# Attention scores with split keys: the second pass over 128 rows, with zeros beside the low parts, in place of a pass over 64

## Chip, core and metric

The kernel runs as one program on one core of a Trainium2 chip. The metric is the time of one execution in device microseconds (us). TensorE (PE in the profile) multiplies matrices; a weight load (PEld) puts the stationary operand in place ahead of each matmul. VectorE (DVE), ScalarE (ACT) and GpSimd (POOL) work on tiles; SyncE (SP) issues nearly all DMAs. A pass here is one matmul instruction with its weight load; its pitch is the time from its start to the start of the next instruction on PE.

## What is computed

Four layers over 512 tokens of width 1024, in fp32: a mixer with short convolution and forgetting attention, a conformer convolution, an HGRN2 mixer and a sliding-window attention, each followed by a feed-forward layer. The change touches the scores of the two attentions. Heads are 64 wide.

```python
# forgetting attention (layer 0): 8 heads, blocks of 128 queries, all earlier keys
s = einsum("bqhd,bkhd->bhqk", q[:, start:end], k[:, :end]) * 64 ** -0.5
s = where(mask, s + bias, -inf); p = softmax(s)
outs.append(einsum("bhqk,bkhd->bqhd", p, v[:, :end]))
...
# sliding window attention (last layer): 16 query heads on 2 key heads, blocks of 128 queries x 256 keys
scores = einsum('bnqkgd,bnskd->bnkgqs', q, kb) * 64 ** -0.5
scores = where(valid, scores - slopes * dist, -inf)
out = einsum('bnkgqs,bnskd->bnqkgd', softmax_with_sink(scores), vb)
```

## The kernel before

**Precision by splitting.** Matmuls run in a rounded 32-bit type. To keep fp32 accuracy a value is split into a high part (the rounded copy) and a low part (value minus copy), and a product takes three passes: high by high, high by low, low by high. `mm3` (lines 537 to 541) does this for all projections: L539, L540 and L541 are its three passes, on tiles named fm, tm and op.

**Scores.** A head has only 64 rows, half of the 128 that a matmul can contract over. So `stack_q` puts, for head i of a pair (i is 0 or 1), the high part of q in one half of the rows and the low part in the other, and `stack_k` copies the high part of k to both halves. `mm_s` then needs two passes:

```python
T.matmul(out, lhsT=q[:, i, qs], rhs=k[:, i, ks], start=True, stop=False)               # L845
T.matmul(out, lhsT=q[HALF[i], i, qs], rhs=kl[HALF[i], ks], start=False, stop=True)     # L846
```

L845 contracts over 128 rows (high q and low q, each by high k). L846 contracts over 64 rows, rows 0 to 63 for i = 0 and 64 to 127 for i = 1 (high q by low k). The low parts of both heads of a pair lie in one tile kl of 128 by 512.

**Attention in layer 0.** `fox_worker` (three of them run interleaved) goes over 8 heads and 4 blocks of queries: `mm_s` into a bank S, bias and maximum on DVE (L940), exponential on ACT (L944), scaling on DVE (L947), transposes on PE (L956, bank PT), high and low copy of the transposed weights (L530 on ACT, L531 on DVE, tile PTs), then the product with v (L973, bank O), and two copies into osb (L979 on ACT, L982 on DVE). When a pair of heads is done, `collect` splits it (L530, L531, tile y) and frees its q, k and kl. Scores are 128, 256, 384 or 512 wide, 8 pairs of passes each. Between these stand the projections of later heads, and at the end the output projection (op), which goes through its weights in units: first the first half of the columns for units 0 to 3, then the second half for units 0 to 2, and so on.

**Sliding window.** `att` does the same for 8 pairs of heads and two halves of the sequence: 8 passes in a row per half (L845 and L846 in turn, 256 wide, or 128 wide at the sequence's start), then bias and maximum on DVE (L1708), exponentials on ACT (L1720), transposes on PE (L1732), copies on ACT (L1734) and the product with v (L1743). There are 64 pairs of passes: 16 of 128 wide and 48 of 256.

**What sets the order.** A planner in the kernel's file (`Sched`) runs all of this as tasks. Each operation has a fixed cost in a formula; the planner takes the one that could start first and emits it, so the order on every engine is fixed when the kernel is built. Buffers come from pools with a fixed number of slots: `spool` has 34 slots of 4 KB per partition, shared by weights, q, k, PTs, y and others, `tpool` has 8 of 2 KB. A weight unit takes three slots in turn: wr (the DMA's target), wh (high part, L498 on ACT) and wl (low part, L507 on DVE). Where the planner expects PE to stand idle for more than 0.6 us, and a bank is free, it puts matmuls of zeros there (`warm`, L1880).

A tile kl comes from `tpool` in layer 0 and from `spool` in the sliding window.

Of the kernel before, what the change touches and what calls it, by code (L numbers as in the profile page):

```python
# [8 lines left out]
F32 = mybir.dt.float32  # L9
F32R = mybir.dt.float32r  # L10
U8 = mybir.dt.uint8
AF = mybir.ActivationFunctionType
ALU = mybir.AluOpType
# [386 lines left out]
def program(nc, tc, ap, tp, debug=None):  # L400
    S = Sched()
    V, A, G, T = nc.vector, nc.scalar, nc.gpsimd, nc.tensor
    spool = Pool(tp["s"], "s", N_SLOTS)
    tpool = Pool(tp["t2"], "t2", N_T2)
# [7 lines left out]
    def dve(n, fn, reads, writes, fast=False, aps=0):  # L412
        return Op("DVE", 0.069 + n * (0.00052 if fast else 0.00104) + 0.061 * aps, fn, reads, writes)

    def act(n, fn, reads, writes, table=None, extra=0.0, psum=False):
        return Op("ACT", (0.05 if psum else 0.093) + n * 0.000833 + extra, fn, reads, writes, table=table)
# [10 lines left out]
    def slot(shape=(128, 1024), dtype=F32, name="s", need=1):  # L427
        return Alloc(spool, list(shape), dtype, name, need=need)
# [7 lines left out]
    def bank(name="b", need=1):  # L436
        return Alloc(ppool, [128, 512], F32, name, need=need)

    def free(*bs):
        for b in bs:  # L440
            b.pool.put(b)
# [70 lines left out]
    def get_w():  # L512
        u = W.cur
        W.cur += 1
        yield Wait(lambda: u in W.lo)
        W.gone += 1
        return W.hi.pop(u), W.lo.pop(u)
# [305 lines left out]

    HALF = (slice(0, 64), slice(64, 128))

    def stack_q(q, b):
        for i in range(2):
            s_, o_ = HALF[i], HALF[1 - i]  # L830
            yield act(512, lambda: A.activation(out=q[s_, i, :], in_=b[s_, :], func=AF.Copy, scale=0.125), (b,), (q,), psum=True)
# [4 lines left out]
    def stack_k(k, kl, b):  # L836
        for i in range(2):
            s_, o_ = HALF[i], HALF[1 - i]
            yield act(512, lambda: A.activation(out=k[s_, i, :], in_=b[s_, :], func=AF.Copy), (b,), (k,), psum=True)
            yield act(512, lambda: A.activation(out=k[o_, i, :], in_=b[s_, :], func=AF.Copy), (b,), (k,), psum=True)  # L840
            yield dve(512, lambda: V.tensor_tensor(out=kl[s_, :], in0=b[s_, :], in1=k[s_, i, :].bitcast(F32), op=ALU.subtract), (b,), (kl,))
        free(b)

    def mm_s(out, q, k, kl, i, qs, ks):
        T.matmul(out, lhsT=q[:, i, qs], rhs=k[:, i, ks], start=True, stop=False)  # L845
        T.matmul(out, lhsT=q[HALF[i], i, qs], rhs=kl[HALF[i], ks], start=False, stop=True)  # L846


    def short_conv(ct, gc, xa, gb, ys):
# [57 lines left out]
    def fox_worker(env, qk, osb, heads, done):  # L907


        for hd in heads:  # L910
# [14 lines left out]
            for pr in range(2):  # L925
# [51 lines left out]
                ts_ = slice(256 * pr, 256 * pr + 256)  # L977
                s_, o_ = HALF[par], HALF[1 - par]
                yield act(256, lambda: A.activation(out=ob[s_, ts_], in_=b2[o_, :256], func=AF.Copy), (b2,), (ob,), psum=True)  # L979
# [27 lines left out]
    def layer0_mixer():  # L1007
        env, qk, osb, ys = {}, {}, {}, {}
        spool.reserve = RES[0] + BASE

        def qk_copy(i, qb_, kb_):
            q = yield slot((128, 2, 512), F32R, "q", need=4)
            yield from stack_q(q, qb_)
            k = yield slot((128, 2, 512), F32R, "k", need=4)
            kl = yield Alloc(tpool, [128, 512], F32R, "kl", need=2)
            yield from stack_k(k, kl, kb_)
            qk[i] = (q, k, kl)

        vv = []

        def v_room():
            for i in range(4):
                vv.append((yield slot((128, 8, 128), F32R, "v", need=4)))

        def v_copy(n, tb, b):
            yield Wait(lambda: len(vv) == 4)
            t = vv[tb]
            src = b[:, :256].rearrange("p (h d) -> p h d", d=64)
            y = [t[:, 4 * n:4 * n + 4, 64 * i:64 * i + 64] for i in range(2)]
            yield from split(src, b, y, t, n=256, psum=True)  # L1030
            free(b)
            if all(x.need <= 0 for x in vv):
                env["v"] = vv

        S.spawn(v_room(), -5, "v")

        def v_part(n, cuts):

            bs, k = [], 0
            for m in cuts:  # L1040
                w = yield from get_w()
                for tb in range(4):
                    if k == 0:
                        bs.append((yield bank("tm", need=8)))
                    b, ts_ = bs[tb], slice(128 * tb, 128 * tb + 128)
                    for i in range(m):
                        ki, cs = k + i, slice(n * i, n * i + n)
                        yield pe(3 * n / 2400, lambda: mm3(b[:, :n], (xh[:, ki, ts_], xl[:, ki, ts_]), (w[0][:, cs], w[1][:, cs]), ki == 0, ki == 7),
                                 [w[0], w[1], X.blocks[tb][ki // 4]], [b])
                free(*w)  # L1050
                k += m
            return bs

        def gates(bs):

            g = yield t2("fg", (128, 4, 8), need=4)
            for tb in range(4):
                yield dve(8, lambda: V.tensor_copy(out=g[:, tb, :], in_=bs[tb][:, 256:264]), (bs[tb],), (g,))
            for tb in range(4):
                S.spawn(v_copy(0, tb, bs[tb]), -5, "v")  # L1060
            b = yield bank("fT")

            def tr():
                for tb in range(4):
                    T.transpose(b[:8, 128 * tb:128 * tb + 128], g[:, tb, :], ident)
            yield pe(0.436, tr, (g, bident), (b,))
            free(g)
            yield from fox_decay(b, env)

        bs = yield from fm_quads(4)  # L1070
        S.spawn(qk_copy(0, bs[0], bs[1]), -5, "qk")
        S.spawn(qk_copy(1, bs[2], bs[3]), -5, "qk")
        bs = yield from v_part(264, (3, 3, 2))
        S.spawn(gates(bs), -6, "decay")
        bs = yield from v_part(256, (4, 4))
        for tb in range(4):
            S.spawn(v_copy(1, tb, bs[tb]), -5, "v")

        left = [2] * 4

        def done(i):
            left[i] -= 1

        for i in range(FOX_WORKERS):
            S.spawn(fox_worker(env, qk, osb, range(i, 8, FOX_WORKERS), done), -4, f"fox{i}")

        def collect(i):
            yield Wait(lambda: left[i] == 0)
            y = osb[i]
            y.need = 0  # L1090
            p = yield slot((128, 2, 512), F32R, "y", need=2)
            yield from split(y.t, y, (p[:, 0, :], p[:, 1, :]), p)
            free(y)
            ys[4 + i] = p
            free(*qk[i], env["nck"][i])
            if sum(left) == 0:
                free(*vv)

        for i in range(4):
            S.spawn(collect(i), -5, f"y{i}")  # L1100
        got = {}
        for n, c in P1_FM_TAIL:
            got[n, c] = yield from fm_unit()
            if n == "k":
                S.spawn(qk_copy(c, got["q", c], got["k", c]), -5, "qk")
            elif n == "gb":
                S.spawn(short_conv(c, got["gc", c], got["xa", c], got["gb", c], ys), -5, "sconv")
        chain, blocks = boundary(B("mix_post0", "ffn_pre0"), "h0m")
        yield from out_proj([lambda k=k: ys.get(k) for k in P2_ORDER], chain, P=PQ[0][0], Q=PQ[0][1])
        X.blocks = blocks  # L1110
# [528 lines left out]
    def swa(kv_blocks_done):  # L1639
        ys, qs, osb, env = {}, {}, {}, {}  # L1640
# [15 lines left out]
        def kv_epi(k, v):  # L1656
            nonlocal vs
            ks = yield slot((128, 2, 512), F32R, "k", need=4)
            s = yield slot((128, 2, 512), F32, "kl", need=1)
            kl = yield slot((128, 512), F32R, "kl", need=2)  # L1660
            env["kv"] = s
            vs = s[:, 1, :].rearrange("p (a b) -> p a b", b=128)
            yield from stack_k(ks, kl, k)
            env["k"], env["klo"] = ks, kl
            t = yield t2("vT")
            yield dve(512, lambda: V.tensor_copy(out=t.t, in_=v.t), (v,), (t,))
            free(v)
            b = yield bank("vt")

            def tr():  # L1670
                for i in range(4):
                    T.transpose(b[:, 128 * i:128 * i + 128], t[:, 128 * i:128 * i + 128], ident)
            yield pe(0.436, tr, (t, bident), (b,))
            free(t)
            yield act(512, lambda: A.activation(out=s[:, 1, :], in_=b.t, func=AF.Copy), (b,), (bv, s), psum=True)
            free(b)
# [92 lines left out]
        for a in range(2, 8):  # L1769
            b = yield from fm_unit()  # L1770
# [174 lines left out]
```

## Time and profile before

| | us |
|---|---|
| median of 3 runs | 2363.87 (2362.8 to 2363.88) |
| the profiled execution | 2366.44 |
| its span | 2364.6 |
| PE busy | 2345.2 (99%) |
| PE weight loads busy | 1979.6 (84%) |
| DVE busy | 1198.5 (51%) |
| ACT busy | 911.8 (39%) |
| POOL busy | 129.3 (5%) |
| share of PE in the chain that ended last | 96% |

Busy time of an engine counts the time that instructions are in it. Matmuls overlap, so a busy PE need not be a PE at its peak: what a matmul costs is read from its pitch, not from its duration.

### The profile page before, as it was taken

What the parts mean: (1) busy time and instruction counts of PE and PEld (TensorE: products, weight loads), DVE (VectorE), ACT (ScalarE), POOL (GpSimd) and SP (SyncE); (2) the same over time, 40 slices, a digit from 0 to 9 for tenths busy, and PEclk for the clock granted to TensorE, in tenths of its full rate; (3) what the DMA queues carried; (4) which work ended last, traced back from release to release, by engine and by line L of the source; (5) the groups of instructions that cost most, each with busy time, mean ns of one, the idle gap of its engine ahead of it and who ended that gap; (6) DMA issues with size and microseconds to landing.
All of it is one profiled execution on the core that took longest, in us unless ns stands there. A gap on an engine that the chain in (4) does not pass through costs nothing.

```text
span 2364.6 us, 29469 instructions
## 1 busy us (share of the span) xinstructions
PE 2345.2 (99%) x11828; PEld 1979.6 (84%) x11828; DVE 1198.5 (51%) x2038; ACT 911.8 (39%) x1614; POOL 129.3 (5%) x152
## 2 busy tenths in 40 slices
PE   9999999999999999999999999999999999999998
PEld 9778988888878988888988889888888788888887
DVE  5776533333787533323656875444345445444432
ACT  6454323222466332322543544333323554333331
POOL 0000000000383000000000000000000000000000
PEclk9999999999999999999999999999999899999999
DMA  5223322232343222233221122222342013222240
GB/s 185 99 73 115 117 72 89 89 130 94 120 149 115 99 81 89 72 125 125 81 98 54 63 97 91 80 77 85 116 151 81 10 46 115 95 75 72 98 143 36
DMA packets 62936, 224.68 MB, mean 95 GB/s; under 512 B 6984, under 2 KB 7240, under 8 KB 62800
## 3 DMA queue, kind: packets, MB, share of 16 engines
q1 hardware_dynamic: 62368, 222.41, 27.4%
q8 instruction: 93, 1.52, 0.3%
q10 hardware_dynamic: 432, 0.40, 0.1%
q14 instruction: 43, 0.35, 0.0%
HBM read 220.67 MB, written 2.11 MB: 94 GB/s over the span
## 4 chain that ended last, share of the span: by engine, by line
PE 96%; DVE 1%; POOL 1%; ACT 1%; DMA 0%; issue 0%; SPq 0%; POOLq 0%; ACTq 0%; DVEq 0%
PE fm L539 18%; PE fm L541 18%; PE fm L540 18%; PE op L539 9%; PE op L541 9%; PE op L540 9%; PE tm L539 2%; PE tm L541 2%; PE tm L540 2%; PE S L846 1%; PE xt L689 1%; PE O L1743 1%; PE S L845 1%; PE S L1506 1%; POOL cy L1188 1%; PE o L1569 1%
## 5 line engine op out<-in xcount | busy, mean ns | idle before, releaser
L539 PE MATMUL fm<-xh,wh 128*128 128x512 f32 (+1 forms) x2160 | 799.6, 370 | 0.0
L541 PE MATMUL fm<-xh,wl 128*128 128x512 f32 (+1 forms) x2160 | 789.2, 365 | 0.0
L540 PE MATMUL fm<-xl,wh 128*128 128x512 f32 (+1 forms) x2160 | 789.2, 365 | 0.0
L507 DVE TENSOR_TENSOR wl<-wr,wh 128x1024 fp32r<-128x1024 f32 x379 | 457.1, 1231 | 286.6 <-ACT wh L498 180.7
L498 ACT ACTIVATE wh<-wr 128x1024 fp32r<-128x1024 f32 x379 | 387.3, 1051 | 261.7 <-DMA wr<-wall 128.4
L541 PEld LDWEIGHTS fm<-xh,wl 128*128 128x128 f32 x2160 | 409.0, 189 | 65.9
L539 PEld LDWEIGHTS fm<-xh,wh 128*128 128x128 f32 x2160 | 409.7, 190 | 65.0 <-issue 2.5
L540 PEld LDWEIGHTS fm<-xl,wh 128*128 128x128 f32 x2160 | 409.7, 190 | 61.4
L539 PE MATMUL op<-wh,p 128*128 128x512 f32 x704 | 274.9, 390 | 0.4 <-DVE sg L805 0.4
L541 PE MATMUL op<-wh,p 128*128 128x512 f32 x704 | 274.0, 389 | 0.0
L540 PE MATMUL op<-wl,p 128*128 128x512 f32 x704 | 273.9, 389 | 0.0
L805 DVE TENSOR_TENSOR sg<-fm,sg 128x512 f32<-128x512 f32 x88 | 60.9, 692 | 383.3 <-PE fm L541 376.2
L530 ACT ACTIVATE p<-sg 128x512 fp32r<-128x512 f32 x88 | 55.6, 632 | 357.4 <-DVE sg L805 357.4
L539 PEld LDWEIGHTS op<-wh,p 128*128 128x128 f32 x704 | 132.2, 188 | 28.2 <-DVE sg L805 0.9
L541 PEld LDWEIGHTS op<-wh,p 128*128 128x128 f32 x704 | 132.1, 188 | 27.5
L540 PEld LDWEIGHTS op<-wl,p 128*128 128x128 f32 x704 | 132.2, 188 | 27.1
L660 POOL TENSOR_TENSOR ss<-ss,mhalf 128x1 f32<-128x1 f32 x48 | 26.1, 543 | 1449.7 <-DVE ss L655 1443.1
L539 PE MATMUL op<-wh,y 128*128 128x512 f32 x256 | 102.8, 402 | 0.2 <-DVE y L1002 0.2
L541 PE MATMUL op<-wh,y 128*128 128x512 f32 x256 | 100.0, 391 | 0.0
L540 PE MATMUL op<-wl,y 128*128 128x512 f32 x256 | 99.8, 390 | 0.0
L531 DVE TENSOR_TENSOR p<-sg,p 128x512 fp32r<-128x512 f32 x88 | 60.9, 693 | 61.4 <-ACT p L530 61.4
L1188 POOL TENSOR_TENSOR cy<-cp,cy 128x512 f32<-128x512 f32 x60 | 86.1, 1436 | 30.1 <-ACT cp L1187 26.1
(246 smaller groups left out, 2277.5 us busy)
## 6 DMA issues: line engine op xcount, KB each, us to landing
wr<-wall SPq DMA_DIRECT2D x379, 512.0 KB, 3.5
row<-rows SPq DMA_DIRECT2D x14, 512.0 KB, 3.7
cm<-cmat SPq DMA_DIRECT2D x14, 512.0 KB, 4.6
h<-x SPq DMA_DIRECT2D x8, 256.0 KB, 7.2
nck<-negc SPq DMA_DIRECT2D x4, 512.0 KB, 5.6
alibi<-alibi SPq DMA_DIRECT2D x4, 512.0 KB, 4.9
out<-out SPq DMA_DIRECT2D x8, 256.0 KB, 2.3
mk<-masks SPq DMA_DIRECT2D x2, 288.0 KB, 5.1
```

The costliest lines, as they stand in the source:

```text
L498: yield act(1024, lambda: A.activation(out=b.t, in_=r.t, func=AF.Copy), (r,), (b,))
L507: yield dve(1024, lambda: V.tensor_tensor(out=b.t, in0=r.t, in1=hh.t.bitcast(F32), op=ALU.subtract), (r, hh), (b,))
L530: yield act(n, lambda: A.activation(out=y0, in_=raw, func=AF.Copy), (rb,), (yb,), psum=psum)
L531: yield dve(n, lambda: V.tensor_tensor(out=y1, in0=raw, in1=y0.bitcast(F32), op=ALU.subtract), (rb,), (yb,))
L539: T.matmul(out, lhsT=a[0], rhs=b[0], start=s, stop=False)
L540: T.matmul(out, lhsT=a[0], rhs=b[1], start=False, stop=False)
L541: T.matmul(out, lhsT=a[1], rhs=b[0], start=False, stop=e)
L660: yield Op("POOL", 0.29 + 0.167 * cols, lambda: G.tensor_tensor(out=ss[:, 8:8 + cols], in0=ss[:, 4:4 + cols], in1=mhalf[:, :cols], op=ALU. ...
L689: T.transpose(b[:, 128 * i:128 * i + 128], n[:, c:c + 128], ident)
L805: yield dve(512, lambda: V.tensor_tensor(out=c.t, in0=u.t, in1=c.t, op=ALU.mult), (u, c), (c,))
L845: T.matmul(out, lhsT=q[:, i, qs], rhs=k[:, i, ks], start=True, stop=False)
L1188: yield pool(512, lambda: G.tensor_tensor(out=y.t, in0=p.t, in1=y.t, op=ALU.add), (p,), (y,))
```

## The change

The tile kl gets two planes like k, one for each head of the pair. The plane of head i holds the low part of k in that head's half of the rows, and zeros in the other half, written by a memset on GpSimd. The second pass of `mm_s` then contracts over all 128 rows, with the same stationary operand as the first; the zeros take out the product with the low part of q. kl doubles in size, and in layer 0 it moves from `tpool` to `spool`.

```diff
     def stack_k(k, kl, b):
...
-            yield dve(512, lambda: V.tensor_tensor(out=kl[s_, :], in0=b[s_, :], in1=k[s_, i, :].bitcast(F32), op=ALU.subtract), (b,), (kl,))
+            yield dve(512, lambda: V.tensor_tensor(out=kl[s_, i, :], in0=b[s_, :], in1=k[s_, i, :].bitcast(F32), op=ALU.subtract), (b,), (kl,))
+            yield Op("POOL", 0.5, lambda: G.memset(kl[o_, i, :].bitcast(F32), 0.0), (), (kl,))
...
     def mm_s(out, q, k, kl, i, qs, ks):
         T.matmul(out, lhsT=q[:, i, qs], rhs=k[:, i, ks], start=True, stop=False)
-        T.matmul(out, lhsT=q[HALF[i], i, qs], rhs=kl[HALF[i], ks], start=False, stop=True)
+        T.matmul(out, lhsT=q[:, i, qs], rhs=kl[:, i, ks], start=False, stop=True)
...
-            kl = yield Alloc(tpool, [128, 512], F32R, "kl", need=2)
+            kl = yield slot((128, 2, 512), F32R, "kl", need=4)
...
-            kl = yield slot((128, 512), F32R, "kl", need=2)
+            kl = yield slot((128, 2, 512), F32R, "kl", need=4)
```

In the changed file the two passes are lines 847 and 848, the memset is line 843, and later lines move by two. The planner makes a new order from it. On PE, DVE and ACT the order differs inside the attention of layer 0 only; in the sliding window no matmul changes its place.

The end of layer 0's attention on PE before: the last scores, the first half of the columns of the output projection for unit 3 (weights 1923 and 1925), transposes, and the last product with v.

```order
L845 MATMUL S_2053<-k_1766,q_1743 128x512
L846 MATMUL S_2053<-kl_1767,q_1743 128x512
...
L541 MATMUL op_2011<-wh_1837,y_1285 128x512
L539 MATMUL op_1975<-wh_1923,y_1566 128x512
L540 MATMUL op_1975<-wl_1925,y_1566 128x512
...
L956 MATMUL PT_2030<-ident,B_2040 128x128 x2
L539 MATMUL op_2000<-wh_1923,y_1566 128x512
...
L541 MATMUL op_2108<-wh_1683,y_1032 128x512
L973 MATMUL O_2110<-PTs_2094,v_92 128x256 x2
```

The same place on PE after (the four op groups of unit 3 now use weights 2129 and 2148):

```order
L847 MATMUL S_2058<-k_1785,q_1757 128x512
L848 MATMUL S_2058<-kl_1786,q_1757 128x512
...
L541 MATMUL op_2011<-wh_1901,y_1258 128x512
L1882 MATMUL warm_2089<-zeros 128x128 x3
L958 MATMUL PT_2026<-ident,B_2036 128x128 x2
...
L1882 MATMUL warm_2104<-zeros 128x128 x9
L975 MATMUL O_2103<-PTs_2097,v_92 128x256 x2
...
L1882 MATMUL warm_2157<-zeros 128x128 x18
L539 MATMUL op_1974<-wh_2129,y_1544 128x512
```

Five op groups of three passes that stood among the last transposes and products now stand behind them, with three runs of warm matmuls in their place.

The end of layer 0's attention on ACT, before: the high part of unit 3's weights (1923) is made well ahead of the last copies.

```order
L530 ACTIVATE PTs_1899<-PT_1848 128x384
L498 ACTIVATE wh_1923<-wr_1921 128x1024
L979 ACTIVATE osb_1786<-O_1907 64x256
...
L979 ACTIVATE osb_1786<-O_2110 64x256
L530 ACTIVATE y_2129<-osb_1786 128x512
L498 ACTIVATE wh_2141<-wr_2139 128x1024
```

On ACT after:

```order
L530 ACTIVATE PTs_2100<-PT_2027 128x384
L981 ACTIVATE osb_1811<-O_2103 64x256
L530 ACTIVATE y_2124<-osb_1811 128x512
L498 ACTIVATE wh_2129<-wr_2127 128x1024
```

The high part of unit 3's weights (2129) now stands behind the last copy of the attention's output and its split.

## Rows read from the trace of the kernel before

**Rows 1.** Busy PE, PEld, DVE, ACT, POOL (x instructions), PEclk, DMA: layer 0's attention, sliding window.
```profile
70.00:200.00 130.00, 129.25 (x613) 100.04 (x612) 100.32 (x293) 61.35 (x135) 0.30 (x3) 1.00 0.27 92
1826.00:1960.00 134.00, 134.00 (x702) 106.66 (x701) 62.33 (x234) 69.28 (x206) 0.00 (x0) 0.91 0.12 40
```
**Rows 2.** PE in order of time, sliding window: start us, duration us, line, tiles, shape.
```profile
1882.24 0.38 PE L846 MATMUL S<-kl,q 64*128 64x256 f32 x1
1882.55 0.38 PE L845 MATMUL S<-k,q 128*128 128x256 f32 x1
1882.86 0.38 PE L846 MATMUL S<-kl,q 64*128 64x256 f32 x1
```
**Rows 3.** PE in order of time, end of layer 0's attention.
```profile
200.92 1.16 PE L973 MATMUL O<-PTs,v 128*128 128x256 f32 x8
201.91 0.45 PE L539 MATMUL op<-wh,y 128*128 128x512 f32 x1
...
205.08 0.48 PE L539 MATMUL op<-wh,y 128*128 128x512 f32 x1
...
207.93 1.05 PE L973 MATMUL O<-PTs,v 128*128 128x256 f32 x8
208.82 0.45 PE L539 MATMUL op<-wh,y 128*128 128x512 f32 x1
```
**Rows 4.** Weight loads in order of time, the block of rows 2: in brackets idle time before.
```profile
1882.24 0.18 PEld L846 LDWEIGHTS S<-kl,q 64*128 64x128 f32 x1 [0.25 <-issue]
```
**Rows 5.** PE in order of time, attention of layer 0, passes of other widths.
```profile
72.32 0.33 PE L846 MATMUL S<-kl,q 64*128 64x128 f32 x1
72.57 0.33 PE L845 MATMUL S<-k,q 128*128 128x128 f32 x1
...
88.73 0.39 PE L541 MATMUL fm<-xh,wl 128*128 128x512 f32 x1
88.96 0.34 PE L845 MATMUL S<-k,q 128*128 128x384 f32 x1
89.23 0.44 PE L846 MATMUL S<-kl,q 64*128 64x384 f32 x1
89.59 0.50 PE L539 MATMUL fm<-xh,wh 128*128 128x512 f32 x1
...
95.92 0.49 PE L846 MATMUL S<-kl,q 64*128 64x512 f32 x1
96.34 0.44 PE L845 MATMUL S<-k,q 128*128 128x384 f32 x1
```
**Rows 6.** Granted clock (PEclk, 1.00 is 2.4 GHz) in two stretches of the sliding window.
```profile
1846.00:1864.00 18.00, 18.00 (x48) 12.73 (x48) 7.63 (x33) 5.21 (x19) 0.00 (x0) 0.53 0.00 0
...
1920.00:1929.00 9.00, 9.00 (x24) 6.15 (x24) 3.81 (x20) 1.37 (x6) 0.00 (x0) 0.62 0.00 0
```
**Rows 7.** PE in order of time inside the first of these stretches.
```profile
1847.28 0.58 PE L846 MATMUL S<-kl,q 64*128 64x256 f32 x1
1847.79 0.58 PE L845 MATMUL S<-k,q 128*128 128x256 f32 x1
```
**Rows 8.** Memsets of 128 by 512 on GpSimd in a later stage: ns min/median/max, first and last start.
```profile
L1448 POOL MEMSET ST<- x8: 522/528/532, 1161.5 to 1367.1; 128x512 f32 x8
```
**Rows 9.** DVE in order of time, end of layer 0's attention.
```profile
203.44 0.48 DVE L947 TENSOR_SCALAR B<-B,sm 128x512 f32<-128x512 f32 x1
205.77 1.16 DVE L531 TENSOR_TENSOR PTs<-PT,PTs 128x512 fp32r<-128x512 f32 x2 [1.85 <-ACT PTs L530]
...
211.51 10.31 DVE L507 TENSOR_TENSOR wl<-wr,wh 128x1024 fp32r<-128x1024 f32 x9 [0.26 <-ACT wh L498]
```
**Rows 10.** Warm matmuls of a later stage, same columns.
```profile
L1880 PE MATMUL warm<-zeros x38: 275/275/275, 735.5 to 739.6; 128*128 128x128 f32 x38
```
**Rows 11.** ACT and PE in order of time: a softmax's last row, and the transposes after it.
```profile
1841.23 0.19 ACT L1720 ACTIVATION_READ_ACCUMULATOR E<-E,sm 128x1 f32 x1
...
1841.90 0.49 PE L1732 MATMUL PT<-ident,E 128*128 128x128 f32 x3
```

## The prediction

> **What bounds the kernel now.** I read the busy times by stretch first. In the attention of layer 0 and in the sliding window PE is in a matmul nearly all the time: 129.25 of 130 us and 134.00 of 134 us, with DVE at 100.3 and 62.3 and ACT at 61.4 and 69.3 [rows 1]. So what PE spends there is time, as long as the other engines can follow. Busy is not fast, though, so the second view is PE in order of time, read by pitch. In the sliding window a pass of 256 columns, L845 or L846, has a pitch of 0.31 us [rows 2]. The product with v at the end of layer 0 also has 128 by 128 weights and 256 columns (128 in its last two passes), and takes 0.89 us for 8 passes (207.93 to 208.82): 0.11 each [rows 3]. The weight loads say why: the one for L846 starts together with its matmul, after 0.25 us in which the loader waited for nothing that the profile shows [rows 4], and its 0.18 us lie open. Passes over the same number of rows have their load hidden. A change from 128 to 64 rows, and the one back, costs each pass some 0.2 us.
>
> **What the second pass over 128 rows takes away.** I take 0.11 us for a pass of up to 256 columns (the row above; no row is lower), 0.17 for 384 (an estimate between 0.11 and 0.23) and 0.23 for 512 (L541 before the scores, 88.73 to 88.96 [rows 5]). Both passes of a pair gain, since both stand behind a change of rows.
> Sliding window: 48 pairs of 256 columns at 2 x 0.31 become 2 x 0.11, so 48 x 0.40 = 19.2 us; 16 pairs of 128 columns at 2 x 0.25 (72.32 to 72.57 [rows 5]; the rows of the window read alike) become 0.22, 16 x 0.28 = 4.5. Sum 23.7.
> Layer 0: L846 has 0.25, 0.31, 0.36 and 0.42 for the four widths [rows 5], 0.14, 0.20, 0.19 and 0.19 over the price after: 0.18 on average. L845 mostly follows a pass over 128 rows, has its load hidden, and loses 0.10 at its end (0.27 against 0.17 at 384 columns, 88.96 to 89.23 [rows 5]). 32 x 0.28 = 9.0 us.
> A rule of the Trainium skill speaks against this. The row of the product with v shows 8 passes on the same 128 rows at 0.11 us, far below a load and a matmul in turn. The Trainium skill (TensorE: Matmul & The Clock Gate, the section on packing small matmuls) says that weight loads overlap running matmuls only when their row groups differ; two passes over all 128 rows share all groups, so by that rule nothing is gained here. The trace disagrees with 0.11 us, and the same page names the background weight buffer as an exception; I sum by the trace.
>
> **The clock.** In two stretches of the sliding window the granted clock falls to its lower level, 1.2 GHz: a mean of 0.53 over 18 us and 0.62 over 9 us [rows 6], which is 18 x 0.47 + 9 x 0.38 = 11.9 us if all work there were twice as long. Both begin inside the only two places where 16 score passes stand in a row, and blocks of 8 did not bring it down. The 20 score passes inside have 0.51 [rows 7], not 0.62, so 20 x 0.055 = 1.1 us less: 10.8 us. After the change those 16 passes take 1.8 us and are as dense as the product with v, in whose runs in layer 0 the clock stays at 1.00 [rows 1]. I take the whole 10.8; the other end is 0.
> Sum of what PE sheds: 23.7 + 9.0 + 10.8 = 43.5 us.
>
> **What it adds.** Ten memsets of 64 by 512 on GpSimd, 0.53 us each by the nearest row [rows 8]. GpSimd is busy 0.3 us in 130 there [rows 1], and in the new order the memsets stand ahead of the subtractions that fill the other half, and no subtraction waits for them; only the scores do. Cost 0; if the cover were gone, at most 2 x 0.53 per pair of heads.
> The four tiles kl in `spool` cost more. They hold slots that weights took before, so the planner puts the high part of unit 3's weights behind the attention's last copies, and PE, which had four op groups of unit 3 and one more between its last transposes and products, has nothing there. Three holes open, each priced by the chain of before.
> First, behind the last scores: their end is at 200.92, L947 is done at 203.44 + 0.48 = 203.92, while PE has only the product (0.99 us) and two groups of 6 x 0.23 us: 3.0 - 2.4 = 0.6 us. Second, from the transposes' end at 205.08 to the end of the copies at 205.77 + 1.16 = 206.93: 1.85 us. Third, from the product's end at 208.82 to the first of nine low parts, 211.51 + 10.31/9 = 212.66; only one pass can go ahead of it: 3.84 - 0.23 = 3.6 us [rows 3, 9]. Sum 6.1 us. The warm matmuls in the holes lengthen nothing: 38 in 4.1 us make 0.11 us each [rows 10], 18 of them 2.0 us in the hole of 3.6.
> Last, waits that are not there now. With 9 us out of 130, DVE in layer 0 goes from 77% to 83% of the time (100.3 of 121) [rows 1]; with 34 out of 134, DVE in the window goes to 62% and ACT to 69%. The order was fixed by the planner, and PE has run behind its chains. Where the slack is small it shows: the last exponential's sum is done at 1841.42 and the transposes start at 1841.90 [rows 11], 0.5 us, and a block of 8 scores in between gets 1.5 us shorter (23.7 us in 16 blocks). So a turn of the softmax can wait about 1 us. If a quarter of the 16 turns do, that is 4 us; I add 3 for layer 0, a third of what PE sheds there. 7 us, with ends at 0 (as now) and 21 (every turn, and over half of layer 0's gain).
>
> **The sum.** 43.5 - 6.1 - 7 = 30.4 us. The profiled execution took 2366.4 us, its span 2364.6, and the three timed ones have a median of 2363.9; the difference of 2.5 is the profile's, so I subtract from the median: 2363.9 - 30.4 = 2333.5, say 2333 us.
>
> **Rivals.**
> *The others can't follow.* DVE in layer 0 and the chain from exponentials to transposes in the window become what PE waits for, at the upper end of the waits. For it: 83% of DVE, and slack of half a microsecond. Against: PE waits nowhere in these stretches now, and ACT and DVE have 30% left in the window. 43.5 - 6.1 - 19 = 18: 2346 us.
> *The clock stays low.* The runs of small matmuls around the scores, not the scores, bring it down. For it: the product with v in the window has only 64 columns a pass. Against: it runs at full clock in all other places. Without the 10.8 us: 2344 us.
> *No holes, no waits.* The weights come earlier than the order suggests and the slack is enough. 2363.9 - 43.5 + 2 = 2322 us.
> *Slower.* The pitch of 0.31 us is not due to the change of rows, for instance since two passes on all rows can't overlap load and matmul. Then nothing is gained, and the holes at the end of layer 0 are left: 2363.9 + 6.1 = 2370 us. It decides when 192 passes gain less than 6.1 us together, 0.03 us each. This is also the case that the change doesn't do what it says. Against: the product with v, and L845 itself, which loses only 0.10 us when it follows a pass over 128 rows and 0.20 when it follows one over 64. The rule cited above, on weight loads and row groups, would give this time; the trace leaves it little.
>
> **How the numbers follow.** Forecast 2333 (2326 to 2339): 0.56. The others can't follow: 0.16. Clock stays low: 0.12. No holes and no waits: 0.12. Slower: 0.04. The range takes in the rivals next to the forecast, 2320 to 2346, and leaves out the slower case and the outer parts of the others. A measurement of this kernel tells about 0.2%, 4.7 us, from no change. All cases but one are faster by more: faster 0.95, within 0.2% 0.01, slower 0.04.
>
> **What would show it.** Right: in the window passes of 256 columns with a pitch of 0.11 to 0.12 us, weight loads without idle time ahead of them, and no stretch under a granted clock of 0.9 there; at the end of layer 0 three waits of PE of about 0.6, 1.9 and 3.6 us, or warm matmuls in their place; new PE waits for L1720's and L947's results, 7 us in all. Wrong: score passes still at 0.31 us (the cause is another), low clock in the same places (the scores were not what brought it down), waits of PE over 20 us in either attention (the other engines bound it), or none at the end of layer 0 (the order tells less than I took from it).

## The result, and the profile after

The changed kernel takes **2328.19 us** (median; 2326.68 to 2328.51) against 2363.39 us for the kernel before in the same comparison: a ratio of 0.9847, with a 95% interval of 0.9835 to 0.9858. That is 35.2 us less, where 30.4 were forecast (2333, range 2320 to 2346). The profiled execution took 2326.68 us with a span of 2324.9 us. In the changed kernel the lines behind the scores stand two further down: the passes are L847 and L848, the scaling on DVE L949, the transposes of layer 0 L958, its product with v L975, the warm matmuls L1882.

Busy times of the whole execution, and then the same two stretches as in [rows 1] (columns as there; the sliding window now begins 6.5 us earlier):

```profile
PE 2306.1 (99%) x11888; PEld 1969.2 (85%) x11888; DVE 1197.4 (52%) x2038; ACT 912.1 (39%) x1614; POOL 134.8 (6%) x162
```
```profile
70.00:200.00 130.00, 129.63 (x704) 110.34 (x704) 106.67 (x306) 68.02 (x146) 2.65 (x7) 1.00 0.30 102
1820.00:1920.00 100.00, 100.00 (x695) 91.04 (x693) 60.23 (x234) 68.65 (x206) 0.00 (x0) 1.00 0.15 54
```

PE is as busy as before and has done the same work in less time: nearly the same 700 matmuls of the sliding window now fit in 100 us, where they took 134. The granted clock is 1.00 in all of it.

The scores of the sliding window, PE and then weight loads in order of time (columns as in [rows 2] and [rows 4]):

```profile
1858.54 0.28 PE L848 MATMUL S<-kl,q 128*128 128x256 f32 x1
1858.66 0.28 PE L847 MATMUL S<-k,q 128*128 128x256 f32 x1
1858.77 0.28 PE L848 MATMUL S<-kl,q 128*128 128x256 f32 x1
```
```profile
1858.42 0.19 PEld L848 LDWEIGHTS S<-kl,q 128*128 128x128 f32 x1
1858.54 0.19 PEld L847 LDWEIGHTS S<-k,q 128*128 128x128 f32 x1
```

The pitch is 0.12 us in place of 0.31. A load takes 0.19 us, as before, but the next one starts 0.12 us after it, beside the matmul that runs: the bracket with idle time of [rows 4] is gone. Both passes of a pair now use the same stationary operand, but it is not loaded once for the two: each pass still has its load. Summed over the 128 passes of the sliding window, the pitches went from 41.3 us to 15.74.

In layer 0 the other widths, answering to [rows 5]:

```profile
71.46 0.27 PE L848 MATMUL S<-kl,q 128*128 128x128 f32 x1
71.57 0.27 PE L847 MATMUL S<-k,q 128*128 128x128 f32 x1
...
86.17 0.35 PE L848 MATMUL S<-kl,q 128*128 128x384 f32 x1
86.35 0.40 PE L539 MATMUL fm<-xh,wh 128*128 128x512 f32 x1
...
93.48 0.39 PE L848 MATMUL S<-kl,q 128*128 128x512 f32 x1
93.70 0.33 PE L847 MATMUL S<-k,q 128*128 128x384 f32 x1
```

128 columns take 0.11 us, 384 take 0.18, 512 take 0.22. The 64 passes together go from 19.8 us to 10.4. The pass that follows the scores gains as well. For the projection pass L539 it is 0.24 us of pitch on average where it had 0.34, some 20 times in layer 0.

The end of layer 0's attention, PE in order of time and then DVE, answering to [rows 3] and [rows 9]:

```profile
190.92 0.83 PE L1882 MATMUL warm<-zeros 128*128 128x128 f32 x6
191.59 0.61 PE L958 MATMUL PT<-ident,B 128*128 128x128 f32 x4
192.04 2.17 PE L1882 MATMUL warm<-zeros 128*128 128x128 f32 x18
193.97 1.13 PE L975 MATMUL O<-PTs,v 128*128 128x256 f32 x8
194.94 4.23 PE L1882 MATMUL warm<-zeros 128*128 128x128 f32 x36
198.92 0.48 PE L539 MATMUL op<-wh,y 128*128 128x512 f32 x1
199.24 0.39 PE L540 MATMUL op<-wl,y 128*128 128x512 f32 x1
```
```profile
191.00 0.49 DVE L949 TENSOR_SCALAR B<-B,sm 128x512 f32<-128x512 f32 x1
192.71 1.16 DVE L531 TENSOR_TENSOR PTs<-PT,PTs 128x512 fp32r<-128x512 f32 x2 [1.22 <-ACT PTs L530]
...
197.61 9.36 DVE L507 TENSOR_TENSOR wl<-wr,wh 128x1024 fp32r<-128x1024 f32 x8 [0.25 <-ACT wh L498]
```

The three holes are there, filled with zeros: 0.67, 1.93 and 3.98 us from the start of the warm matmuls to the start of what follows. In the last one the high and low parts of unit 3's weights are late: the first low part is done at 197.61 + 9.36/8 = 198.78, L539 (which needs the high part) starts at 198.92 and L540 (which needs the low part) at 199.24. And this is all that PE waits for in layer 0's attention by the view of waits (engine, tile and line waited for: us, times, longest); in the sliding window that view has no line:

```profile
PE PT L958 <- DVE B L949: 0.4, 1, 0.4
```

### The profile page after: what moved, and what is told of

Read it like the earlier page. It is cut to its first block, busy times and chain, and to the rows that moved or that the text cites. A ratio compares the mean times of both kernels' runs of the same rounds, so it can differ in the third digit from the quotient of the medians.

```text
span 2324.9 us, 29594 instructions
## 1 busy us (share of the span) xinstructions
PE 2306.1 (99%) x11888; PEld 1969.2 (85%) x11888; DVE 1197.4 (52%) x2038; ACT 912.1 (39%) x1614; POOL 134.8 (6%) x162
## 4 chain that ended last, share of the span: by engine, by line
PE 95%; POOL 1%; DVE 1%; ACT 1%; issue 1%; DMA 0%; SPq 0%; POOLq 0%; ACTq 0%
PE fm L539 18%; PE fm L540 18%; PE fm L541 18%; PE op L539 9%; PE op L541 9%; PE op L540 9%; PE tm L539 2%; PE tm L541 2%; PE tm L540 2%; POOL cy L1190 1%; PE xt L689 1%; PE O L1745 1%; PE S L1508 1%; PE o L1571 1%; PE PT L1734 1%
## 5 line engine op out<-in xcount | busy, mean ns | idle before, releaser
L539 PE MATMUL fm<-xh,wh 128*128 128x512 f32 (+1 forms) x2160 | 794.8, 368 | 0.0
L540 PE MATMUL fm<-xl,wh 128*128 128x512 f32 (+1 forms) x2160 | 787.3, 364 | 0.2 <-DVE xl L699 0.2
L539 PEld LDWEIGHTS fm<-xh,wh 128*128 128x128 f32 x2160 | 408.3, 189 | 61.7
L540 PEld LDWEIGHTS fm<-xl,wh 128*128 128x128 f32 x2160 | 408.3, 189 | 61.4 <-DVE xl L699 0.4
L539 PE MATMUL op<-wh,p 128*128 128x512 f32 x704 | 274.9, 390 | 0.4 <-DVE sg L805 0.4
L540 PE MATMUL op<-wl,p 128*128 128x512 f32 x704 | 273.9, 389 | 0.0
L539 PEld LDWEIGHTS op<-wh,p 128*128 128x128 f32 x704 | 132.1, 188 | 28.1 <-DVE sg L805 0.9
L540 PEld LDWEIGHTS op<-wl,p 128*128 128x128 f32 x704 | 132.2, 188 | 27.0
L539 PE MATMUL op<-wh,y 128*128 128x512 f32 x256 | 102.7, 401 | 0.2 <-DVE y L1004 0.2
L540 PE MATMUL op<-wl,y 128*128 128x512 f32 x256 | 99.8, 390 | 0.0
```

The source lines that it names most:

```text
L539: T.matmul(out, lhsT=a[0], rhs=b[0], start=s, stop=False)
L540: T.matmul(out, lhsT=a[0], rhs=b[1], start=False, stop=False)
```

## The experiments

The theory: a pass lies open with its weight load (0.19 us) where the number of rows changes; PE's lower clock in the sliding window comes from the scores standing at that slow pitch; the larger buffers cost some 6 us at the end of layer 0. The rivals are given with each run.

**The two places apart.** `mm_s` and `stack_k` take a flag, so that one attention has the new second pass and the larger tile, and the other is as before.

```diff
-    def mm_s(out, q, k, kl, i, qs, ks):
+    def mm_s(out, q, k, kl, i, qs, ks, wide):
...
+        if wide:
+            T.matmul(out, lhsT=q[:, i, qs], rhs=kl[:, i, ks], start=False, stop=True)
+        else:
+            T.matmul(out, lhsT=q[HALF[i], i, qs], rhs=kl[HALF[i], ks], start=False, stop=True)
```

Sliding window alone:

> Only the sliding window has the second pass over 128 rows; layer 0 is the kernel before, order and tiles. Theory (a change of rows lays the weight load open, and runs of 16 such passes bring the clock down): score passes of the window at 0.11 to 0.13 us, granted clock 1.00 all through the window, no holes at the end of layer 0; 23.7 us of pitch and 10.8 us of clock less, some 33 us in all by the profile of the changed kernel: 2330 us. Rival (the low clock comes from PE's state when it leaves layer 0 or from other stages): two stretches at about 0.55 stay and the time is 2338 to 2341 us.

Measured 2332.97 us, ratio 0.9873 (0.9859 to 0.9886): 30.5 us less than the 2363.47 of before, and 3 us above the 2330 expected, which went by one profiled execution of each kernel. Layer 0 alone:

> Only layer 0 has the second pass over 128 rows, with the tiles kl in the larger pool and so the new order; the sliding window is the kernel before. Theory: 9.4 us of score pitch and about 2 us behind the scores gained, 6.6 us given back in three holes at the end of layer 0's attention: 5 us less, 2358 us, and the two stretches of low clock in the window stay. Rival (the profile's holes were filled with work that PE would have done anyway, so they cost nothing): 2352 us.

Measured 2358.61 us, ratio 0.9976 (0.9963 to 0.9988): 4.9 us less. The two add up to 35.4, the whole gain of 35.2, so no run shows that one place depends on the other. The second term is the less certain: its interval is 2.8 to 8.7 us, and its executions reach from 2354.84 to 2364.59 us, since the low clock of the unchanged sliding window is longer in some than in others (30.7 us in all in the profiled one, at 2364.59, against 23.9 in that of the kernel before). In layer 0 the sum of its parts is 9.4 from the scores, some 2 from the pass behind them, less 6.6 of holes: 4.8.

**The buffers without the passes.** The larger tile, the memsets and the order that follows from them, but the second pass over 64 rows.

```diff
-        T.matmul(out, lhsT=q[:, i, qs], rhs=kl[:, i, ks], start=False, stop=True)
+        T.matmul(out, lhsT=q[HALF[i], i, qs], rhs=kl[HALF[i], i, ks], start=False, stop=True)
```

> All of the change but the wide pass: kl with two planes, memsets and the new order, while the second pass stays on 64 rows. Same matmuls in the same order as the changed kernel. Theory (the holes at the end of layer 0 are set by the chain from the last scores to unit 3's weights, whatever the scores cost): holes of 0.5, 1.9 and 4.0 us, 2363.4 + 6 = 2369 to 2370 us. Rival (the holes only open since PE got faster): 2363 to 2365 us. Also: score passes at 0.25 to 0.42 us as before, and the low clock at its two places.

Measured 2368.01 us, ratio 1.0020 (1.0012 to 1.0029): 4.5 us slower than before (2.8 to 6.9), 1 to 2 us less than expected. The same three groups of warm matmuls stand in its trace (6, 18 and 36 matmuls from 201.45, 202.56 and 205.46 on). So the holes are there with the slow passes too: the change buys its gain with about 5 us, and the order of instructions by itself gives nothing back.

**One slot less held back.** The weights of layer 0 must leave a number of slots of `spool` free; one less lets unit 3's weights in earlier.

```diff
-RES = (8, 15, 8, 4)
+RES = (7, 15, 8, 4)
```

> The changed kernel with one number altered: 7 slots of the large pool instead of 8 are held back from the weights in layer 0. In the order that follows unit 3's weights stand ahead of the attention's last copies again and no warm matmuls stand at the end of layer 0. Theory: the three holes (6.6 us) close and nothing else changes: 2328.2 - 6.6 = 2321.6 us. Rival (one slot less for the attention makes PE wait elsewhere in layer 0, or the last copies bound the stage anyway): 2326 to 2330 us, with waits of PE in layer 0.

Measured **2322.51 us**, ratio 0.9829 (0.9815 to 0.9842), 5.7 us below the changed kernel, and the fastest version of this study. No warm matmul is left in layer 0's attention, and the view of waits has two lines in place of the three holes:

```profile
PE op L539 <- DVE osb L984: 0.9, 1, 0.9
PE op L539 <- DVE PTs L531: 0.6, 1, 0.6
```

6.6 us of holes have become 1.5 us of waits. The holes were a matter of slots, as the prediction had read from the order, and not of DVE or ACT being too slow.

**The holes without the zeros.** The planner puts no warm matmuls at the end of layer 0.

> The changed kernel without the three runs of warm matmuls at the end of layer 0's attention. Theory (the chain sets the holes, the warm matmuls only fill them): PE waits there 0.6, 1.9 and 3.7 us, 6 us in all, and the time stays within 1 us of 2328 unless the clock falls in the last hole. Rival (the warm matmuls are longer than the chain and make part of the holes): waits of 4 to 5 us in all and 2326 us.

Measured 2328.15 us, ratio 0.9841 (0.9824 to 0.9857), as the changed kernel. PE's waits there, in order of time with the idle time in brackets, and the granted clock of the two stretches around them:

```profile
191.59 0.66 PE L958 MATMUL PT<-ident,B 128*128 128x128 f32 x4 [0.46 <-DVE B L949]
192.77 0.38 PE L975 MATMUL O<-PTs,v 128*128 128x256 f32 x1 [0.53 <-ACT PTs L530]
193.50 1.59 PE L975 MATMUL O<-PTs,v 128*128 128x256 f32 x7 [0.34 <-DVE PTs L531]
197.62 0.79 PE L539 MATMUL op<-wh,y 128*128 128x512 f32 x1 [2.53 <-ACT wh L498]
198.88 0.79 PE L540 MATMUL op<-wl,y 128*128 128x512 f32 x1 [0.47 <-DVE wl L507]
```
```profile
186.00:198.00 12.00, 8.14 (x41) 6.36 (x39) 5.98 (x14) 5.42 (x11) 0.00 (x0) 0.82 0.40 137
198.00:204.00 6.00, 5.53 (x13) 4.05 (x13) 6.00 (x6) 5.32 (x6) 0.00 (x0) 0.50 0.00 0
```

The holes are the chain's, not the zeros': ACT starts the high part of unit 3's weights at 196.53 here and at 196.54 in the changed kernel. But they are not the waits of the expectation. The idle times come to 3.9 us, and 0.5 more ahead of L540, where 6 were expected; that is the sum that the rival named, though not its 2326 us. For PE is at its lower clock from about 193.7 to 204.0, from ahead of the last hole. The product with v fills part of the hole by taking longer, and the passes behind it have a pitch of 0.43 us where L539 has 0.23. The zeros keep the clock at 1.00, and what they lengthen is 0.36 us: L540 starts at 199.24 behind them and at 198.88 without them. Layer 0 ends 2.1 us later in this trace than in that of the changed kernel, but the medians don't differ. The profiled execution of the changed kernel lies 1.5 us under its median and this one 1.1 us above its own, so what the zeros are worth in a typical execution stays open.

**The passes doubled.** Every score pass of the sliding window runs twice, in each kernel; the second run starts the bank anew, so the scores are the same. What stands in the loop is moved in by one level.

```diff
+                    for again in range(2):
                     for nb in (2 * n2, 2 * n2 + 1):
```

> The kernel before with every block of score passes in the sliding window issued twice in a row (the second run overwrites the first with the same values), so that every block has 16 passes or more. 128 passes more, 96 x 0.31 + 32 x 0.25 = 38 us at full clock. Theory (long runs of passes with open weight loads bring the clock down): the clock falls to 1.2 GHz in most of the 14 places, mean granted clock of the window under 0.85; 2363 + 38 + 20 or more, over 2420 us. Rival (the two places of before have the low clock for another reason, such as the matmuls around): low clock in two places only, 2363 + 38 + 5 = 2406 us or less.

> The changed kernel with every block of score passes in the sliding window issued twice in a row, as in the run of the kernel before with it. 128 passes more at 0.12 us are 15 us. Theory: the passes are dense, the clock stays at 1.00 through the window, 2328 + 15 = 2343 us. Rival (the number of score passes in a row brings the clock down, dense or not): stretches of low clock in the window, 2350 us or more.

Measured 2444.24 us, ratio 1.0332 (1.0311 to 1.0354), and 2342.15 us, ratio 0.9900 (0.9881 to 0.9920). 128 more passes cost the kernel before 78.7 us, 0.61 each, and the changed kernel 14.0 us (against its 2328.19), 0.11 each. Of the 0.61 the pitch of [rows 2] is 0.31; the rest is the clock. A stretch of the sliding window in the doubled kernel before, then in the doubled changed kernel (the granted clock stands third from the end):

```profile
1860.00:1880.00 20.00, 20.00 (x48) 12.82 (x48) 4.73 (x22) 1.97 (x8) 0.00 (x0) 0.50 0.00 0
```
```profile
1860.00:1880.00 20.00, 20.00 (x157) 18.99 (x156) 11.71 (x51) 12.88 (x46) 0.00 (x0) 1.00 0.17 54
```

More of the slow passes bring the clock down for longer (it is low for 122.9 us of the sliding window, where it was 23.9), and more of the dense ones don't bring it down at all. That rules out the rival by which the small products around the scores did it: they are the same in both.

**Same passes, other order.** Is it the 64 rows that are slow, or the change of rows? Here the kernel before keeps its 64-row passes and buffers, and each block of the sliding window has its four full passes first and its four 64-row passes after them. One part of the computation is changed by it: both full passes of a bank start it, and some low passes don't add to the sums.

```diff
-                    for nb in (2 * n2, 2 * n2 + 1):
+                    for lo in range(2):
                         for i in range(2):
+                            for nb in (2 * n2, 2 * n2 + 1):
```

> The kernel before with the 8 score passes of a block of the sliding window in another order: the 4 passes over 128 rows first, then the 2 over rows 0 to 63, then the 2 over rows 64 to 127. Same passes, same results, 64-row passes kept. Theory (the change of rows costs, not the 64 rows): only the passes at a change have 0.25 to 0.31 us, 2 or 3 of 8; the others have 0.11; 16 blocks get 1.0 to 1.2 us shorter, 16 to 19 us, and if the runs get dense enough the clock stays up, 8 to 11 us more: 2334 to 2347 us. Rival (a pass over 64 rows is slow in itself, and holds up the pass behind it): all four L846 passes stay at 0.31 us, only three L845 passes of a block gain 0.2: 9.6 us, 2354 us with the low clock, 2343 without.

Measured 2334.32 us, ratio 0.9868 (0.9853 to 0.9882): nearly what the wide pass gives in the sliding window, with all the 64-row passes still there. The same order with only the first full pass of a bank starting it, so that every low pass is added:

> The grouped order again, four full passes of a block and then its four 64-row passes, with the kernel before's 64-row passes and buffers, and with every low pass added, as in the kernel before: only the first full pass of a bank starts it. Theory (the order sets the time, and what is added does not): 2334 us, within 2 of the first grouped run, and 16.8 us for the 128 window passes. Rival (the first grouped run was quick because some low passes replaced the sums): 2338 us or more.

Measured 2335.85 us, ratio 0.9879 (0.9864 to 0.9894); 16.8 us for the 128 passes. It is the change of rows. Nor does the gain come from the stationary operand that both passes share in the changed kernel: here each kind of pass has its own.

**Changes in pairs.** Half as many changes: for each block of 128 queries two full passes, then two 64-row passes.

```diff
                         for i in range(2):
-                            mm_s(b[i][:, ...], q, env["k"], env["klo"], i, ...)
+                            T.matmul(b[i][:, ...], lhsT=q[:, i, qs_], rhs=env["k"][:, i, ks_], start=True, stop=False)
+                        for i in range(2):
+                            T.matmul(b[i][:, ...], lhsT=q[HALF[i], i, qs_], rhs=env["klo"][HALF[i], ks_], start=False, stop=True)
```

> The kernel before, with its 64-row second pass and its old buffers; only the sliding window's passes stand in pairs: for each block the full passes of head 0 and head 1, then their two 64-row passes, so a change of the row count comes before every second pass in place of every pass. The sums are those of the kernel before. Theory (a weight load lies open where the row count changes, about 0.19 us each in the kernel before, 0.31 against 0.12): 64 of 128 changes go, 64 times 0.19 = 12.2 us: 2351 us if the stretches at a low clock stay as they were, down to 2344 if they go as they did where only the window was made wide. Rival (the run with four full and four 64-row passes owed its 2334 to what it left out, the adding of some low passes, and not to the fewer changes): within 2 us of 2363.5.

Measured 2340.2 us, ratio 0.9900 (0.9883 to 0.9916): 4 us less than the lower end of the theory. A block of 8 passes of 256 columns took 1.40 us, where 8 x 0.12 and three changes inside it at 0.19 us would make 1.53, and 1.72 with the one at its end (1867.67 to 1869.07 in the rows below). Either the price of a change isn't fixed, or something else got cheaper: in this order two 64-row passes that use different halves of the rows follow each other. So the same number of changes once more, but head by head:

> The kernel before, with its 64-row second pass; in the sliding window the passes stand head by head: the two full passes of head 0, its two 64-row passes, then the same for head 1. As in the run in pairs the row count changes before every second pass (4 times per 8 passes), but two 64-row passes in a row now use the same half of the rows, where there they used different halves. The sums are those of the kernel before. Theory A (the number of changes decides): the block of 8 passes of 256 columns stays at 1.40 us and the time at 2340 us, within 2. Theory B (two 64-row passes in different halves of the rows run beside each other, which made the pairs cheaper than 0.19 us per change): two passes per block, 0.12 us each, come back, 1.64 us per block, 16 blocks of it 3.8 us: 2344 us.

Measured 2351.46 us, ratio 0.9947 (0.9935 to 0.9959). PE in order of time in one block, and the load of one pair of 64-row passes; first for the order of heads, L1701 full and L1699 over 64 rows:

```profile
1874.99 0.39 PE L1701 MATMUL S<-k,q 128*128 128x256 f32 x2
1875.32 0.50 PE L1699 MATMUL S<-kl,q 64*128 64x256 f32 x2
1875.75 0.50 PE L1701 MATMUL S<-k,q 128*128 128x256 f32 x2
1876.18 0.50 PE L1699 MATMUL S<-kl,q 64*128 64x256 f32 x2
1876.61 0.55 PE L1735 MATMUL PT<-ident,E 128*128 128x128 f32 x3
```
```profile
1876.18 0.29 PEld L1699 LDWEIGHTS S<-kl,q 64*128 64x128 f32 x2
```

then for the order in pairs, L1698 full and L1700 over 64 rows:

```profile
1867.67 0.40 PE L1698 MATMUL S<-k,q 128*128 128x256 f32 x2
1868.01 0.39 PE L1700 MATMUL S<-kl,q 64*128 64x256 f32 x2
1868.32 0.51 PE L1698 MATMUL S<-k,q 128*128 128x256 f32 x2
1868.76 0.38 PE L1700 MATMUL S<-kl,q 64*128 64x256 f32 x2
1869.07 0.55 PE L1734 MATMUL PT<-ident,E 128*128 128x128 f32 x3
```
```profile
1868.75 0.19 PEld L1700 LDWEIGHTS S<-kl,q 64*128 64x128 f32 x2
```

Two passes between two changes take 0.43 us: 2 x 0.12 + 0.19. The first two full passes, with a change only behind them, take 0.33. So the price of a change lies half in the pitch ahead of it and half in the pitch behind it, some 0.1 us each, and a block with three changes inside and one at its end should take 8 x 0.12 + 3.5 x 0.19 = 1.62 us. That is what the order of heads took (1874.99 to 1876.61), near theory B's 1.64. Only the 64-row pairs in different halves take 0.31: their two loads lie in the same 0.19 us, and the two matmuls run beside each other. Both pairs together account for the 1.40. The two orders differ in one thing more: two 64-row passes of one head also write to the same bank, and those of two heads to different ones, so these runs don't tell the half from the bank. The time did not follow the block: 2351.5 in place of 2344. The 7 us are the clock's, which falls again in this order and not in the order in pairs. The two stretches of the sliding window with a granted clock under 1.00, and the same part of the order in pairs:

```profile
1845.00:1865.00 20.00, 20.00 (x88) 16.42 (x89) 8.93 (x37) 10.83 (x34) 0.00 (x0) 0.74 0.00 0
...
1905.00:1925.00 20.00, 20.00 (x101) 15.98 (x100) 9.31 (x41) 8.31 (x29) 0.00 (x0) 0.91 0.03 8
```
```profile
1845.00:1865.00 20.00, 20.00 (x129) 17.03 (x128) 13.26 (x48) 14.69 (x43) 0.00 (x0) 1.00 0.01 1
```

20 x 0.26 + 20 x 0.09 = 7.0 us.

**Four 64-row passes in another order.** In the grouped run the heads of the four 64-row passes were 0, 0, 1, 1; here they are 0, 1, 0, 1.

> The grouped order once more (four full passes of a block, then its four 64-row passes; 64-row passes and buffers of the kernel before, the same sums), but the 64-row passes go head 0, head 1, head 0, head 1, so that each is followed by one in the other half of the rows; in the grouped run before it was head 0, head 0, head 1, head 1. Theory (two 64-row passes in different halves run beside each other): the four 64-row passes take as long as two, and one more pass of 0.12 us is saved than in the grouped order before, where only the middle two could overlap: a block of 256 columns goes from 1.01 to 0.89 us, the 128 window passes from 16.8 to 14.9 us, the time from 2335.9 to about 2334 us. Rival (nothing runs beside anything; a 64-row pass is just a little cheaper in some orders): 1.01 us per block and 16.8 us as before.

Measured 2334.49 us, ratio 0.9866 (0.9850 to 0.9883), and 16.8 us for the 128 passes, not 14.9. The four 64-row passes of a block, first with the heads in turn, then as 0, 0, 1, 1:

```profile
1865.86 0.50 PE L1699 MATMUL S<-kl,q 64*128 64x256 f32 x4
1866.30 0.55 PE L1735 MATMUL PT<-ident,E 128*128 128x128 f32 x3
```
```profile
1867.66 0.51 PE L1699 MATMUL S<-kl,q 64*128 64x256 f32 x4
1868.10 0.55 PE L1735 MATMUL PT<-ident,E 128*128 128x128 f32 x3
```

Both take 0.44 us: 0.19 for the change and 2 x 0.12. So four passes take the time of two in either order, and what failed was the expectation that the order 0, 0, 1, 1 could overlap only its middle two. A narrower view, in each run of the last two of the four, shows that both start 0.22 us behind the first; the first two start together as well (1865.864 and 1865.868; 1867.663 and 1867.670):

```profile
1866.09 0.28 PE L1699 MATMUL S<-kl,q 64*128 64x256 f32 x2
```
```profile
1867.89 0.28 PE L1699 MATMUL S<-kl,q 64*128 64x256 f32 x2
```

The passes run two and two in either order. Since two passes of one head don't overlap in the order of heads, the two that start together must be of different heads, in 0, 0, 1, 1 too. Which head a row belongs to isn't in it, so that last step is argued.

## Why the prediction was right, point by point

**What bounds the kernel.** Right. PE was busy throughout both attentions before and after, and each microsecond taken from its passes was one of time: the doubled passes of the changed kernel cost about their pitch, 14.0 us by the medians for 128 passes whose pitches add up to 15.0 in the trace.

**The change of rows.** Right, and now shown and not only argued: by reordering alone, with all 64-row passes kept, 128 passes fall from 41.3 to 16.8 us. Window scores: forecast 23.7 us, measured 25.6, of which 3.5 is passes that stood at the low clock before (at [rows 2] and [rows 5] the 128 passes are 37.8 us and not 41.3). Layer 0: forecast 9.0, measured 9.4, and 2 more that the prediction overlooked, the projection pass behind the scores, which also stood behind a change of rows. The step left out was to ask who follows the 64-row pass, besides L845: L539 behind it starts at 89.59 [rows 5] and the next pass at 89.93, a pitch of 0.34 us, where the prediction took 0.23 for 512 columns.
The trace had decided rightly against the rule that the prediction cites, by which weight loads overlap only across different row groups: 0.12 us of pitch with loads of 0.19 us on the same 128 rows. The Trainium skill (TensorEngine Tiling (Array Packing), Key Properties) has a rule that fits what the runs show: changing the tiling mode drains TensorE. The runs show a price of 0.19 us per change between 128 and 64 rows; the draining itself stands in no row.

**The clock.** Right in kind: no stretch under 1.00 is left in the sliding window. The size of 10.8 us was read from one execution, which lay 2.5 us above the median and had more of the low clock than most. The prediction took these 2.5 us for the profile's; they are not, for the profiled execution of the changed kernel lies 1.5 us under its median. By the medians the sliding window gave 30.5 us, and 25.6 of it are the scores; what is left, 4.9, with the part of the 25.6 that was passes at the low clock, is what the clock gave back in a typical execution. In the two profiled executions the sliding window is 32.9 us shorter, against 23.7 + 10.8 = 34.5.

**The memsets.** Right at 0: no engine waits for them in either attention, and POOL is now busy for 2.65 us in layer 0's.

**The holes.** Forecast 0.6, 1.85 and 3.6 us, measured 0.67, 1.93 and 3.98, in the same places and behind the same chains. The statement that the warm matmuls lengthen nothing was wrong by 0.36 us: the 18 that the planner puts into the last hole are 36 in the trace at 0.11 us each, 3.98 us, not 18 at 2.0 us, so they end just behind the weights' low part. They also do what was not in the prediction: without them PE falls to its lower clock ahead of the last hole.

**New waits.** This is the term that failed: 7 us forecast, 0.4 us measured, and none in the sliding window. The slack of 0.5 us behind one exponential [rows 11] was real, but it did not shrink. The same place after the change, ACT and then PE:

```profile
1832.05 0.19 ACT L1722 ACTIVATION_READ_ACCUMULATOR E<-E,sm 128x1 f32 x1
```
```profile
1832.70 0.49 PE L1734 MATMUL PT<-ident,E 128*128 128x128 f32 x3
```

It is 0.46 us, and was 0.48. The step that failed is the block of 8 scores in between: the softmax's chain starts where its own scores end, and in this turn no other score pass stands on PE between there and its transposes, so faster scores move both ends of the slack alike. How much slack the other turns had was not worked out. DVE at 82% of layer 0's attention (106.67 of 130 us) still kept ahead.

**How the errors add up.** Window: 4 us of waits too many, and 4 us too many for scores and clock together (34.5 against the 30.5 measured by the medians). That these two cancel is luck. Layer 0: 3 us of waits too many, 2.4 of gain too few, holes 0.5 too small, together 4.9 us. The forecast was 4.8 us too high.

**The rivals.** *The others can't follow* falls with the waits. *The clock stays low* falls with the windows at 1.00 and with the doubled passes. *Slower* needed a pitch that stayed at 0.31. *No holes, no waits* (2322) is half right: no waits, but holes; with the holes taken out by one slot, the time is 2322.5.

## What to carry to other kernels

In this kernel a TensorE pass that contracts over fewer rows than its neighbours is paid for at the change and not in itself. Where a kernel has such passes, look at the weight load ahead of them, and either fill up the rows with zeros, or put the passes of one kind together, which here gave nearly the same in one place without any memory. Passes that alternate cost twice where PE's clock falls with them, so read the granted clock of such a stretch together with its pitch. And price the memory that such a change takes, in the order that the planner makes of it: 5 us went there, and one number brought them back.

## What the runs showed of the hardware

The price of a change between 128 and 64 rows was 0.19 us in every order in which it could be read, about half of it ahead of the change and half behind. It is also the duration of a load. Two 64-row passes in different halves of the rows, on different banks, run beside each other: 0.31 us for two with their change, 0.44 for four, and 0.43 for two in the same half and on the same bank. The Trainium skill (TensorE: Matmul & The Clock Gate, the section on packing small matmuls) tells of such overlap of different row groups, and these rows agree with it. Even so no order with 64-row passes came below the zeros in the rows: 16.8 us for the 128 passes of the sliding window at best, against 15.74.

PE's clock fell to its lower level in stretches where the profile shows PE busy 100% of the time, and in places where score passes with changes of rows stand in a row: a granted clock of 0.53 [rows 6], 0.50 in the doubled kernel before, 0.74 with two passes per change on the same half, 1.00 with the same number of changes and 64-row passes side by side. Executions of the kernel before differ by this: in one comparison from 2360.24 us at a mean clock of 0.996 to 2368.75 us at 0.991, while those of the changed kernel lay within 1.8 us.
